# High part of the raw weight operands on VectorE instead of ScalarE, in fifteen pairs of a hybrid decoder layer

## The chip, the cores and the metric

The kernel runs on one core of one Trainium2 chip. The metric is device time in microseconds of one execution. Engines are named as in the profile: PE (TensorE matmuls) with PEld (its weight loads), DVE (VectorE), ACT (ScalarE), POOL (GpSimd) and SP, whose queue issues most of the DMAs. ACT and POOL issue some DMAs too.

## The reference

One layer over 1024 tokens of width 1024, in float32:

```
h = rmsnorm(x)
z_ssm, xBC, dt, q, k, v, f, z_att, g_ssm, g_att = split(h @ w_in)
A = chunked state-space scan over conv(xBC), gated by silu(z_ssm), group norm
B = causal attention with forgetting bias, times silu(z_att)
merged = sigmoid(g_ssm) * (A @ w_branch_ssm) + sigmoid(g_att) * (B @ w_branch_att)
out = x + rmsnorm(merged @ w_out)
```

The work of the matmuls is the four projections: `w_in` (9248 columns), the two branch matrices and `w_out`.

## The kernel before, in words

**Precision.** A float32 product is made of three matmuls on a rounded type: each operand is split into a high part (rounded) and a low part (what is left), and high x high, high x low and low x high are summed in PSUM. For weights this is `Pair.split`: the high part `op[:, 0]` is a copy with rounding, made by ACT (L355), and the low part `op[:, 1]` is source minus high part, made by DVE (L357). Both are 128 x 512 elements and lie in one buffer `wop`, of which there are four.

**Pairs.** The projections are done in units of 128 columns, two units at a time: a `Pair`. Its weights are four blocks `a11`, `a12`, `a21`, `a22` (unit, half of the 1024 rows), loaded by SP's DMAs into `raw` (six buffers, L348). The result of a pair comes from seven products of 12 matmuls each, in the manner of Strassen: steps 1, 2, 4 use a block as loaded (`a11`, `a12`, `a22`), steps 6, 5, 7, 3 use sums of blocks that DVE (POOL in some late pairs) adds first into `sum` (L364, L380) or back into `raw` (L388). So a name `wop<-raw` in the profile stands for steps 1, 2, 4, and for step 7 of those pairs that add in place. The other operands (`x0h`, `x0l` and so on) are blocks of the activations, split in the same way once per phase.

**What sets the order.** `Stream` holds one list of steps, and each call of `half` puts out half a step, 6 matmuls, on PE. The operand of a step is prepared three steps ahead (`ahead`). Results leave PSUM through ACT (L412, a copy that later steps add; L420) and DVE (L422, L424, L426). Around this run the other stages: the recurrence of four groups up to about 640 us, and attention from about 665 to 1130 us. Attention has 41 visits: scores (PE, tile `s`), row minimum with bias (DVE, L1558, into `ex`), exponential (ACT, L1563), transposes (PE, tile `pt`), copies out of PSUM (ACT L1602, DVE L1600), weighted sums (PE, tile `av`). At 24 places a small transpose `tp` (L133) follows, which waits for the first L1558 of its visit, since it takes the PSUM bank that this one reads. PE keeps the program's order exactly; on the other engines a scheduler places the instructions, and each engine then works through its own list in order. Marked calls (`pin`) keep their order.

**The pairs that the change touches** are `late` (four `za`, three `gs`, four `ga`: the gates of attention, of the recurrence's branch and of the attention branch) and `ends[:4]` (the products of the recurrence's branch with `w_branch_ssm`). They run from about 585 us to 1100 us, beside the end of the recurrence and most of attention.

## Time and profile before

| | us |
|---|---|
| median of 3 runs | 1289.95 (1289.72 to 1295.53) |
| the profiled execution's own time | 1288.93 |
| its span, first to last instruction | 1287.2 |
| PE busy | 1247.7 (97%) |
| DVE busy | 1018.2 (79%) |
| ACT busy | 796.8 (62%) |
| POOL busy | 285.8 (22%) |

PE is busy nearly all the time. Its matmuls overlap, so a busy PE may still lose a little between two of them. What the other engines do costs time only where PE has to wait for it, and such waits are listed by the profile's view of waits. A row of a group gives count, busy time, mean duration in ns, and the idle time of that engine just before the group's instructions with what ended it.

### The profile page before, as it was taken

What the parts mean: (1) busy time and instruction counts of PE and PEld (TensorE: products, weight loads), DVE (VectorE), ACT (ScalarE), POOL (GpSimd) and SP (SyncE); (2) the same over time, 40 slices, a digit from 0 to 9 for tenths busy, and PEclk for the clock granted to TensorE, in tenths of its full rate; (3) what the DMA queues carried; (4) which work ended last, traced back from release to release, by engine and by line L of the source; (5) the groups of instructions that cost most, each with busy time, mean ns of one, the idle gap of its engine ahead of it and who ended that gap; (6) DMA issues with size and microseconds to landing.
All of it is one profiled execution on the core that took longest, in us unless ns stands there. A gap on an engine that the chain in (4) does not pass through costs nothing.

```text
span 1287.2 us, 21110 instructions
## 1 busy us (share of the span) xinstructions
PE 1247.7 (97%) x7066; PEld 986.4 (77%) x7066; DVE 1018.2 (79%) x1979; ACT 796.8 (62%) x1728; POOL 285.8 (22%) x307
## 2 busy tenths in 40 slices
PE   6999999999999999899999999999999999999998
PEld 4787888788887888688777777777777777678886
DVE  6998888798789888788677766776778877976976
ACT  8745666566556656566556666666667656753753
POOL 0000330024102320134001222222111212346052
PEclk9999999999999999999999999999999999999999
DMA  7332543545363554545475664656587657665932
GB/s 282 100 107 71 159 143 125 195 140 151 131 188 122 151 175 145 142 131 152 149 256 173 214 215 163 238 197 210 193 279 279 219 187 248 238 210 198 369 114 101
DMA packets 154669, 233.60 MB, mean 181 GB/s; under 512 B 17216, under 2 KB 62656, under 8 KB 154560
## 3 DMA queue, kind: packets, MB, share of 16 engines
q1 hardware_dynamic: 142016, 205.53, 49.3%
q0 software_dynamic: 6400, 16.10, 3.3%
q10 hardware_dynamic: 6144, 10.62, 2.2%
q8 instruction: 56, 0.92, 0.3%
q14 instruction: 53, 0.43, 0.1%
HBM read 162.99 MB, written 72.34 MB: 183 GB/s over the span
## 4 chain that ended last, share of the span: by engine, by line
PE 62%; DVE 12%; DMA 9%; issue 7%; ACT 6%; SPq 2%; POOL 1%; ACTq 0%; DVEq 0%; POOLq 0%
PE pb L130 27%; PE pc L130 15%; PE pd L130 5%; PE pt L133 3%; PE av L130 3%; PE s L130 3%; DVE wop L357 3%; PE yps L130 2%; PE tr L133 1%; DVE ex L1558 1%; PE st L130 1%; ACT ex L1563 1%; ACT wop L355 1%; DMA xt<-in_x 1%; DVE sum L364 1%
## 5 line engine op out<-in xcount | busy, mean ns | idle before, releaser
L357 DVE TENSOR_TENSOR wop<-sum,wop 128x512 fp32r<-128x512 f32 x174 | 137.0, 789 | 59.5 <-ACT wop L355 59.1
L355 ACT ACTIVATE wop<-sum 128x512 fp32r<-128x512 f32 x174 | 108.8, 626 | 99.3 <-DVE sum L364 45.3
L1563 ACT ACTIVATE ex<-ex,nm 128x512 f32<-128x512 f32 (+1 forms) x192 | 116.0, 605 | 55.2 <-DVE nm L1558 54.8
L412 ACT ACTIVATE s<-pb 128x512 f32<-128x512 f32 x141 | 83.6, 593 | 101.8 <-PE pb L130 89.5
L357 DVE TENSOR_TENSOR wop<-raw,wop 128x512 fp32r<-128x512 f32 x149 | 114.5, 770 | 35.6 <-ACT wop L355 35.4
L130 PE MATMUL pc<-x3h,wop 128*128 128x512 f32 x384 | 131.2, 398 | 3.1 <-ACT wop L355 1.7
L130 PE MATMUL pb<-x0h,wop 128*128 128x512 f32 x384 | 132.6, 401 | 0.7 <-ACT x0h L1253 0.5
L130 PE MATMUL pc<-x2h,wop 128*128 128x512 f32 x384 | 131.8, 400 | 0.0
L130 PE MATMUL pb<-x5h,wop 128*128 128x512 f32 x376 | 128.0, 397 | 1.9 <-ACT s L412 1.9
L130 PE MATMUL pb<-x6h,wop 128*128 128x512 f32 x376 | 128.3, 397 | 1.1 <-ACT s L412 1.1
L130 PE MATMUL pb<-x4h,wop 128*128 128x512 f32 x376 | 127.6, 397 | 0.3 <-DVE wop L357 0.3
L1558 DVE CUSTOM_DVE_ANT_0 ex<-s,fb 128x512 f32<-128x512 f32 (+1 forms) x192 | 96.4, 552 | 12.2 <-PE s L130 12.1
L355 ACT ACTIVATE wop<-raw 128x512 fp32r<-128x512 f32 x151 | 94.0, 624 | 19.2 <-PE pc L130 11.2
L130 PE MATMUL pd<-x1h,wop 128*128 128x512 f32 x264 | 89.1, 396 | 0.0
L130 PEld LDWEIGHTS pc<-x3h,wop 128*128 128x128 f32 x384 | 72.1, 188 | 21.1 <-ACT wop L355 3.4
L130 PEld LDWEIGHTS pb<-x0h,wop 128*128 128x128 f32 x384 | 72.9, 190 | 17.4 <-ACT x0h L1253 1.5
L130 PEld LDWEIGHTS pc<-x2h,wop 128*128 128x128 f32 x384 | 72.1, 188 | 16.5 <-issue 1.5
L130 PEld LDWEIGHTS pb<-x5h,wop 128*128 128x128 f32 x376 | 70.6, 188 | 18.2 <-ACT s L412 3.0
L130 PEld LDWEIGHTS pb<-x6h,wop 128*128 128x128 f32 x376 | 70.6, 188 | 16.6 <-ACT s L412 1.5
L130 PEld LDWEIGHTS pb<-x4h,wop 128*128 128x128 f32 x376 | 70.5, 188 | 16.0 <-issue 0.7
L214 POOL TENSOR_TENSOR wd<-wd 128x256 f32<-128x256 f32 x32 | 31.7, 990 | 225.9 <-DMA wd<-in_wo 124.7
L130 PE MATMUL pb<-x0l,wop 128*128 128x512 f32 x192 | 75.7, 394 | 0.7 <-DVE x0l L1255 0.7
(341 smaller groups left out, 3000.9 us busy)
## 6 DMA issues: line engine op xcount, KB each, us to landing
raw<-in_wu SPq DMA_DIRECT2D x128, 256.0 KB, 3.7
csb<-cs_dram SPq DMA_DIRECT2D x32, 256.0 KB, 5.0
fb<-f_dram SPq DMA_DIRECT2D x16, 512.0 KB, 6.1
rb<-st_dram SPq DMA_DIRECT2D x48, 128.0 KB, 3.5
wd<-in_wo SPq DMA_DIRECT2D x40, 128.0 KB, 3.1
xt<-in_x SPq DMA_DIRECT2D x8, 512.0 KB, 5.9
gs_dram<-th ACTq DMA_DIRECT2D x16, 256.0 KB, 3.5
qh_dram<-th SPq DMA_DIRECT2D x16, 256.0 KB, 5.0
```

Source lines behind the costliest of these rows:

```text
L130: return tc.keep_in_program_order(nc.tensor.matmul(*args, **kw))
L133: return tc.keep_in_program_order(nc.tensor.transpose(out_, in_, idn))
L214: pin(nc.gpsimd.tensor_tensor(t[out_], t[a_], t[b_], ALU.subtract))
L355: nc.scalar.activation(op[:, 0], src, AF.Copy, scale=sign)
L357: nc.vector.tensor_tensor(op[:, 1], src, op[:, 0], ALU.subtract)
L364: self.adds.tensor_tensor(t, x, y, ALU.add)
L412: nc.scalar.activation(s, ps, AF.Copy)
L1558: nc.vector.tensor_tensor_reduce(to, bank(u, e), fb[hp, h][:, e, 0 : w[u]], 1.0, 3.0e38, ALU.add, ALU.min, nm)
L1563: nc.scalar.activation(to, to, AF.Exp, scale=-1.0, bias=nm, accum_out=hd.at(hd.sm, i, h, e))
```

## The change

In fifteen pairs (the eleven of `late` and `ends[:4]`) the high part of steps 1, 2 and 4 is made by a copy on DVE in place of the copy on ACT. That is 45 instructions of 128 x 512 elements that leave ACT and 45 that come to DVE; the low part stays on DVE, and everything else is as before.

```diff
@@ Pair.__init__
             self.raw, self.op, self.prepared = {}, {}, set()
+            self.alone = False
             self.s1, self.sums, self.closing = None, 0, None
@@ Pair.split
             with urgent:
-                nc.scalar.activation(op[:, 0], src, AF.Copy, scale=sign)
+                if self.alone and which in (1, 2, 4):
+                    nc.vector.tensor_copy(op[:, 0], src)
+                else:
+                    nc.scalar.activation(op[:, 0], src, AF.Copy, scale=sign)
                 if sign == 1.0:
                     nc.vector.tensor_tensor(op[:, 1], src, op[:, 0], ALU.subtract)
@@ after the list of pairs
     ends[-1].closing = closings[7]
+    for p in late + ends[:4]:
+        p.alone = True
```

The scheduler places the new copies and moves some neighbours. PE's and POOL's lists are the same as before. The changed file is longer, so its line numbers are higher by 4 to 6 from `split` on (the copy is its L357, the low part L361, the row minimum L1564).

The first place is DVE's list where attention's visit at 990 us begins, before:

```order
L364 TENSOR_TENSOR sum_10878<-raw_10529,raw_10531 128x512
L282 TENSOR_TENSOR x3l_10380<-x3l_10380,x3h_10379 128x512
L1600 COPY p_10705<-pt_10694 128x256
L282 TENSOR_TENSOR x3l_10380<-x3l_10380,x3h_10379 128x512
L1600 COPY p_10715<-pt_10696 128x256
L357 TENSOR_TENSOR wop_10665<-raw_10297,wop_10665 128x512
L422 TENSOR_TENSOR th_10668<-pc_10671,s_10462 128x512
L357 TENSOR_TENSOR wop_10726<-raw_10152,wop_10726 128x512
L1103 SCALAR_TENSOR_TENSOR th_10668<-th_10669,th_10668 128x512
L1558 ISA ex_6559,nm_10082<-s_10739,fb_10032 128x512
```

And with the change:

```order
L357 CAST wop_10665<-raw_10297 128x512
L368 TENSOR_TENSOR sum_10878<-raw_10529,raw_10531 128x512
L361 TENSOR_TENSOR wop_10665<-raw_10297,wop_10665 128x512
L282 TENSOR_TENSOR x3l_10380<-x3l_10380,x3h_10379 128x512 x2
L1606 COPY p_10705<-pt_10694 128x256
L1606 COPY p_10715<-pt_10696 128x256
L426 TENSOR_TENSOR th_10668<-pc_10671,s_10462 128x512
L357 CAST wop_10726<-raw_10152 128x512
L1107 SCALAR_TENSOR_TENSOR th_10668<-th_10669,th_10668 128x512
L361 TENSOR_TENSOR wop_10726<-raw_10152,wop_10726 128x512
L1564 ISA ex_6559,nm_10082<-s_10739,fb_10032 128x512
```

The operand `wop_10665`, copy and low part, now stands ahead of the two `x3l` rows; the copy of `wop_10726` stands between them and the row minimum.

The second place is the same list some 15 us later, ahead of the next row minimum, before:

```order
L364 TENSOR_TENSOR sum_10880<-sum_10878,raw_10297 128x512
L388 TENSOR_TENSOR raw_10297<-raw_10297,raw_10529 128x512
L357 TENSOR_TENSOR wop_10882<-sum_10880,wop_10882 128x512
L357 TENSOR_TENSOR wop_10965<-raw_10299,wop_10965 128x512
L380 TENSOR_TENSOR sum_10880<-sum_10880,raw_10299 128x512
L1558 ISA ex_6559,nm_10901<-s_10907,fb_10689 128x512
```

And with the change:

```order
L368 TENSOR_TENSOR sum_10880<-sum_10878,raw_10297 128x512
L392 TENSOR_TENSOR raw_10297<-raw_10297,raw_10529 128x512
L357 CAST wop_10965<-raw_10299 128x512
L361 TENSOR_TENSOR wop_10882<-sum_10880,wop_10882 128x512
L361 TENSOR_TENSOR wop_10965<-raw_10299,wop_10965 128x512
L384 TENSOR_TENSOR sum_10880<-sum_10880,raw_10299 128x512
L1564 ISA ex_6559,nm_10901<-s_10907,fb_10689 128x512
```

One row more stands ahead of the row minimum, and nothing has left.

The third place is SP's queue near 977 us, with what each DMA waits for (DMAHW0 to DMAHW7 are eight lanes that the DMAs take in turn; a DMA waits for the one before it on its lane), before:

```order
L1684 DMA x_10691<-t1_a_124 128x512 [waits DMAHW3_49,DMASW0_49]
L1397 DMA q_10683<-qh_dram_87 128x256 [waits DMAHW4_49,PE_49]
L1397 DMA q_10683<-ql_dram_88 128x256 [waits DMAHW6_49]
L1404 DMA k_10686<-kh_dram_89 128x512 [waits DMAHW7_49]
L1404 DMA k_10686<-kl_dram_90 128x512 [waits DMAHW0_49]
L1406 DMA fb_10689<-f_dram_78 128x2x512 [waits DMAHW1_49,DVE_49]
L348 DMA raw_10729<-in_wbs 128x512 [waits DMAHW2_49,Activation_49]
```

And with the change:

```order
L1690 DMA x_10691<-t1_a_124 128x512 [waits DMAHW3_49,DMASW0_49]
L349 DMA raw_10729<-in_wbs 128x512 [waits DMAHW5_49,DVE_49]
L1403 DMA q_10683<-qh_dram_87 128x256 [waits DMAHW6_49,PE_49]
L1403 DMA q_10683<-ql_dram_88 128x256 [waits DMAHW7_49]
L1410 DMA k_10686<-kh_dram_89 128x512 [waits DMAHW0_49]
L1410 DMA k_10686<-kl_dram_90 128x512 [waits DMAHW1_49]
L1412 DMA fb_10689<-f_dram_78 128x2x512 [waits DMAHW2_49,DVE_49]
```

The load of the weight block stands ahead of the loads of `q`, `k` and `fb`, and lane 2 is now that of `fb`.

## The prediction

> **What bounds the kernel now.** I read the page's first part, then the sums of the stage that the change touches (585 to 1102 us), then PE's waits there, and last the stretches of the timeline around those waits.

> ```profile
> span 1287.2 us, 21110 instructions
> PE 1247.7 (97%) x7066; PEld 986.4 (77%) x7066; DVE 1018.2 (79%) x1979; ACT 796.8 (62%) x1728; POOL 285.8 (22%) x307
> ...
> core 0: us, PE busy (x) PEld busy (x) DVE busy (x) ACT busy (x) POOL busy (x), PEclk, DMA share, GB/s
> 585.00:1102.00 517.00, 507.97 (x3333) 393.31 (x3333) 382.85 (x904) 329.67 (x786) 109.20 (x143) 1.00 0.63 210
> ```

> PE sets the end. In these 517 us it is idle for 517.00 - 507.97 = 9.0 us, and that is the most that anything on DVE and ACT can give back here, except for what overlapping matmuls hide. DVE has 134 us free (74% busy), ACT 187 us (64%). What PE waits for, in the same stretch (total, times, longest):

> ```profile
> PE tp L133 <- DVE nm L1558: 4.7, 6, 1.7
> PE pb L130 <- ACT s L412: 1.2, 1, 1.2
> PE s L130 <- ACT p L1602: 1.0, 1, 1.0
> PE pt L133 <- ACT ex L1563: 0.9, 3, 0.3
> PE s L130 <- DVE p L1600: 0.6, 1, 0.6
> ```

> No row names a weight operand: none comes late. Over half of the idle time is one place, the small transpose `tp`, which needs the first row minimum L1558 of its visit. So the question is whether DVE reaches that L1558 earlier or later.

> **The change part by part.** Removed from ACT are 45 copies, added to DVE are 45 (fifteen pairs, steps 1, 2, 4). The groups in the same stretch, the number of DVE's waits from the view of the tile `raw` (total, times), and the two nearest rows for a copy on DVE, over the whole run:

> ```profile
> L355 ACT ACTIVATE wop<-raw 128x512 fp32r<-128x512 f32 x61 | 38.2, 626 | 12.3 <-PE pc L130 11.2 <-PE pd L130 1.1
> ...
> L357 DVE TENSOR_TENSOR wop<-raw,wop 128x512 fp32r<-128x512 f32 x61 | 53.7, 881 | 32.6 <-ACT wop L355 32.6
> ...
>   ACT wop L355: 32.6, 24
> ...
> L1243 DVE TENSOR_SCALAR xt<-xt,rstd 128x512 f32<-128x512 f32 x2 | 0.9, 482 | 0.0
> ...
> L1600 DVE COPY p<-pt 128x512 f32<-128x512 f32 x32 | 21.9, 683 | 5.9 <-PE pt L133 5.9
> ```

> ACT loses 45 x 0.626 = 28 us. PE's waits on ACT (L412, L1602, L1563) total 3.1 us, and none follows one of the removed copies directly, so I count nothing for it; half of it at best would be 1.5 us.

> The copy's price on DVE lies between two rows: 0.482 us (one source, SBUF to SBUF) and 0.683 us (a copy, but out of PSUM). The new one has one source and both ends in SBUF, so I take 0.48. Rows on DVE overlap by 0.08 to 0.09 us (below, L357 at 1006.89 and the next row but one at 1008.10: two rows of 0.69 take 1.21), which leaves 0.40 in line, or 0.60 at the upper end. [...] No run here shows this copy with the rounded type as its result.

> 45 x 0.40 = 18 us come to DVE, against 32.6 us in which it stood idle before 24 of the 61 such low parts (45 of them change), waiting for ACT's copy. Where it stood idle, the copy goes into the wait. The clearest case is the visit at 817.88, ACT's rows, then DVE's, then PE's:

> ```profile
> 818.04 0.60 ACT L412 ACTIVATE s<-pb 128x512 f32<-128x512 f32 x1
> 818.52 0.64 ACT L355 ACTIVATE wop<-raw 128x512 fp32r<-128x512 f32 x1
> ...
> 819.19 0.69 DVE L357 TENSOR_TENSOR wop<-raw,wop 128x512 fp32r<-128x512 f32 x1 [1.20 <-ACT wop L355]
> 819.80 0.68 DVE L1558 CUSTOM_DVE_ANT_0 ex<-s,fb 128x512 f32<-128x512 f32 x1
> ...
> 819.60 0.87 PE L130 MATMUL av<-p,v 128*64 128x256 f32 x8
> 820.55 0.27 PE L133 MATMUL tp<-ident,ns 128*8 128x128 f32 x1
> ```

> DVE is free from 819.19 - 1.20 = 817.99; ACT first does L412. A copy on DVE could run at once and L1558 come 0.7 us earlier. PE gains only the gap between 820.47 and 820.55: **-0.08 us**. That is the pattern of most visits: what DVE gains lies ahead of work that PE wasn't waiting for.

> Where DVE had no idle time, a copy pushes L1558 back by 0.40. It costs PE time only where L1558 already came last. Three places have both. The first is the visit at 665 us, where PE waits for exponentials that follow L1558:

> ```profile
> 667.79 0.69 DVE L357 TENSOR_TENSOR wop<-sum,wop 128x512 fp32r<-128x512 f32 x1
> 668.40 0.69 DVE L357 TENSOR_TENSOR wop<-raw,wop 128x512 fp32r<-128x512 f32 x1
> ...
> 669.60 0.68 DVE L1558 CUSTOM_DVE_ANT_0 ex<-s,fb 128x512 f32<-128x512 f32 x1
> ...
> 671.90 0.33 PE L133 MATMUL pt<-ident,ex 128*128 128x128 f32 x1 [0.34 <-ACT ex L1563]
> ```

> The copy stands ahead of the first of these rows: **+0.40**. The second place is 988 to 1009 us, the two pieces of DVE's list that the section on the change shows:

> ```profile
> 989.44 0.69 DVE L282 TENSOR_TENSOR x3l<-x3l,x3h 128x512 fp32r<-128x512 f32 x1 [3.19 <-ACT x3h L281]
> ...
> 991.32 0.68 DVE L357 TENSOR_TENSOR wop<-raw,wop 128x512 fp32r<-128x512 f32 x1
> ...
> 993.72 0.68 DVE L1558 CUSTOM_DVE_ANT_0 ex<-s,fb 128x512 f32<-128x512 f32 x1
> ...
> 983.30 0.39 PE L130 MATMUL pb<-x4h,wop 128*128 128x512 f32 x1
> ...
> 994.46 0.27 PE L133 MATMUL tp<-ident,ns 128*8 128x128 f32 x1 [0.89 <-DVE nm L1558]
> ...
> 1006.89 0.69 DVE L357 TENSOR_TENSOR wop<-raw,wop 128x512 fp32r<-128x512 f32 x1
> ...
> 1008.10 0.68 DVE L1558 CUSTOM_DVE_ANT_0 ex<-s,fb 128x512 f32<-128x512 f32 x1
> ...
> 1008.85 0.27 PE L133 MATMUL tp<-ident,ns 128*8 128x128 f32 x1 [1.67 <-DVE nm L1558]
> ```

> The first operand (L357 at 991.32) moves into the 3.19 us of idle time before 989.44: its buffer was last read by the product whose last matmul starts at 983.30 (four buffers, four operands back). So 0.60 leaves the run of work ahead of 993.72 and one copy (0.40) enters: -0.20 at 994.46. Before 1008.10 another copy enters: +0.40. Together **+0.20**. The 3.19 us themselves come from ACT, whose store waited for the weight load on lane 2 of the DMAs:

> ```profile
> 988.29 0.60 ACT L412 ACTIVATE s<-pb 128x512 f32<-128x512 f32 x1 [3.90 <-DMA raw<-in_wbs]
> ```

> That load now goes out ahead of `q`, `k` and `fb`, but lane 2 is then that of `fb`, which is issued last and is no smaller, so I expect the same wait and count nothing. The third place is the visit at 1057:

> ```profile
> 1057.08 0.69 DVE L422 TENSOR_TENSOR th<-pc,s 128x512 f32<-128x512 f32 x1 [0.97 <-DMA ms_dram<-th]
> 1057.74 0.69 DVE L357 TENSOR_TENSOR wop<-raw,wop 128x512 fp32r<-128x512 f32 x1
> 1058.95 0.68 DVE L1558 CUSTOM_DVE_ANT_0 ex<-s,fb 128x512 f32<-128x512 f32 x1
> ...
> 1059.70 0.27 PE L133 MATMUL tp<-ident,ns 128*8 128x128 f32 x1
> ```

> Here ACT made its copy beside L422; now it follows on DVE: **+0.40**. It is so at other places behind L422 too (ACT's 12.3 us of waits for PE before these copies are theirs), but there `tp` has room. The copy waits for PE's release of its buffer in DVE's queue; L422 ahead of it waits for the same product, so nothing new is held up.

> Sum: -0.08 + 0.40 + 0.20 + 0.40 = **+0.9 us** (with 0.60 per copy: -0.08 + 0.60 + 0.60 + 0.60 = +1.7). The profiled execution took 1288.93, so 1289.8 by this; the median of the runs shown stands 1.0 above it, which gives 1290.9, say **1291**. The bounds of the sum alone, with half of PE's waits on ACT gained at one end, are 1289 to 1292.

> **Rivals.**

> *A. PE's waits go away.* For it: 32.6 us of DVE's waits and 28 us of ACT's work vanish, and 8.4 us of PE's idle time hang on these two engines. Against it: the clear case above gives PE 0.08, the waits ahead of most late L1558 aren't waits for a removed copy, and the longest of them (1.67) gets a copy more ahead of it. Half of it gives 1290 - 4.2 = 1285.8, all of it 1281.6. Chance 0.17.

> *B. VectorE becomes the bound: slower.* It is the busier of the two (79% against 62%). 37 of the 61 low parts found no wait, by share 37/61 x 45 = 27 of the copies. If each of these pushed PE by its price, as happens from the point where DVE has no idle time left in a visit, that is 27 x 0.40 = 11 us, or 16 at 0.60: 1301 to 1306. Against it are DVE's 134 free us. [...] By the trace DVE is not saturated in the mean. Chance 0.09.

> *C. Copies meet POOL.* Some low parts are stretched while POOL works:

> ```profile
> 802.93 3.24 DVE L357 TENSOR_TENSOR wop<-raw,wop 128x512 fp32r<-128x512 f32 x1
> ...
> 803.08 1.30 POOL L1649 TENSOR_TENSOR y<-y,zr 128x512 f32<-128x512 f32 x1
> 804.33 1.29 POOL L214 TENSOR_TENSOR x<-x,th 128x512 f32<-128x512 f32 x1
> ```

> The group's mean, 881, is 0.19 us above the undisturbed 690. The same for 45 copies is 9 us on DVE, of which by the share of critical places (4 of 24) and some luck 2 to 4 reach PE: 1293 to 1295. Against it: a copy that takes the collision spares the low part behind it. [...] Chance 0.14.

> **How the numbers follow.** The forecast has 0.58, A 0.17, C 0.14, B 0.09, and 0.02 are left for what I don't see. A measurement of this kernel tells a change from none at about 0.5%, 6.4 us: faster means under 1283.5, slower over 1296.4. Only the upper third of A is faster: 0.05. Slower is B and the tail of C: 0.10. The range, 1286 to 1297, leaves out A's better half and B.

> **What would show it.** Right: copies of 0.40 to 0.50 us; the row "DVE wop L357 <- ACT wop L355" loses over half of its time in this stretch; PE's idle time there stays within 8 to 11 us, with `tp` near 1009 us the longest wait. Wrong: copies of 0.68, or stretched to over 1 us in most visits; PE's waits on L1558 grow in number past ten (B); or the 1.2 us behind L412 are gone, when the DMA lane did matter.

## The result, and the profile after

| | before | after |
|---|---|---|
| median (22 runs each) | 1291.34 us (1287.41 to 1296.62) | 1295.71 us (1291.58 to 1300.48) |
| ratio after / before, 95% interval | | 1.0033 [1.0023, 1.0043] |
| the profiled execution's own time | 1288.93 | 1297.97 |

The change made the kernel slower by about 4.3 us. That is under the 0.5% that the prediction took as the bound, and inside its range of 1286 to 1297. The direction is certain nevertheless, and the size is about five times the sum of +0.9. (The forecast of 1291 stood on a median of three runs, 1289.95; on the median of 22 runs the same sum gives 1292.2.)

The first part of the page of the kernel after, then its sums between 585 and 1102 us:

```profile
span 1296.0 us, 21080 instructions
PE 1252.3 (97%) x7066; PEld 988.1 (76%) x7066; DVE 1032.0 (80%) x2024; ACT 771.9 (60%) x1683; POOL 288.8 (22%) x307
...
core 0: us, PE busy (x) PEld busy (x) DVE busy (x) ACT busy (x) POOL busy (x), PEclk, DMA share, GB/s
585.00:1102.00 517.00, 503.52 (x3299) 389.93 (x3296) 389.21 (x931) 299.63 (x727) 104.81 (x137) 0.99 0.63 208
```

ACT is busy for 24.9 us less over the span, DVE for 13.8 us more. PE's idle time in this stretch went from 9.0 to 517.00 - 503.52 = 13.5 us, above the 8 to 11 that the prediction allowed, and PE is also busy for longer over the span with the same 7066 matmuls (1252.3 against 1247.7). Over half of the second lies in the stretch at half clock that item 3 below counts: PE is busy there for 5.57 us with work that took 3.08 before. PE's waits in the same stretch (total, times, longest):

```profile
PE tp L133 <- DVE nm L1564: 6.3, 7, 2.0
PE pt L133 <- ACT ex L1569: 2.7, 3, 1.3
PE pb L130 <- ACT s L416: 1.5, 1, 1.5
PE s L130 <- DVE p L1606: 1.5, 2, 1.1
...
```

The waits for exponentials (`pt`) went from 0.9 to 2.7 us, still three of them: all lie in the visit at 665 us. How far PE is behind itself, instruction by instruction (start after minus start before), shows where the time went. When that visit begins it is 1.37 us, and first scores lie anywhere between 664.7 and 667.0 us in the profiles below whether or not the kernel loses, so I don't count this. In the next visit's scores the shift is 6.0 to 6.1 us. From there to 1067 us it grows by only 1.7 us more, to 7.8, and by 1102 us it is 9.1. These are two single executions, the one before 2.4 us under its kernel's median and the one after 2.3 us over it, so not all of these 9.1 us belong to the change.

The visit at 665 us in the timeline after, DVE's rows, then ACT's, then PE's:

```profile
667.27 0.69 DVE L675 SCALAR_TENSOR_TENSOR th<-th 128x512 f32<-128x512 f32 x1 [2.50 <-ACT th L674]
668.04 0.69 DVE L368 TENSOR_TENSOR sum<-raw 128x512 f32<-128x512 f32 x1
...
670.10 0.42 DVE L357 CAST wop<-raw 128x512 fp32r<-128x512 f32 x1
670.44 0.69 DVE L361 TENSOR_TENSOR wop<-sum,wop 128x512 fp32r<-128x512 f32 x1
...
672.25 0.68 DVE L1564 CUSTOM_DVE_ANT_0 ex<-s,fb 128x512 f32<-128x512 f32 x1
...
673.69 0.71 ACT L1569 ACTIVATE ex<-ex,nm 128x512 f32<-128x512 f32 x1
674.40 0.57 ACT L424 ACTIVATE th<-pb 128x512 f32<-128x512 f32 x1
674.87 0.62 ACT L359 ACTIVATE wop<-raw 128x512 fp32r<-128x512 f32 x1
675.39 0.60 ACT L1569 ACTIVATE ex<-ex,nm 128x384 f32<-128x384 f32 x1
...
666.70 0.97 PE L130 MATMUL s<-k,q 64*128 64x512 f32 x6
...
673.84 0.33 PE L133 MATMUL pt<-ident,ex 128*128 128x128 f32 x1 [1.04 <-ACT ex L1569]
...
676.14 3.21 PE L133 MATMUL pt<-ident,ex 128*128 128x128 f32 x12 [1.27 <-ACT ex L1569]
681.84 1.76 PE L130 MATMUL s<-k,q 64*128 64x512 f32 x12
```

And what answers to these rows in the kernel before, beside the ones that the prediction shows:

```profile
665.19 0.69 DVE L364 TENSOR_TENSOR sum<-raw 128x512 f32<-128x512 f32 x1 [1.78 <-DMA raw<-in_wu]
...
665.33 0.97 PE L130 MATMUL s<-k,q 64*128 64x512 f32 x6
...
672.50 0.33 PE L133 MATMUL pt<-ident,ex 128*128 128x128 f32 x1 [0.27 <-ACT ex L1563]
673.10 1.42 PE L133 MATMUL pt<-ident,ex 128*128 128x128 f32 x11 [0.27 <-ACT ex L1563]
...
675.85 1.65 PE L130 MATMUL s<-k,q 64*128 64x512 f32 x12
```

Counted from the visit's first scores (665.33 and 666.70), the next visit's scores begin at 10.52 and at 15.15 us. Three things make up these 4.6 us:

1. The row minimum stood at 4.27 us and stands at 5.55: +1.28. The first sum began at -0.14 and now begins at 1.34, since its weight block lands 1.35 us later. That gives +1.48. The product L675, which stood behind this sum, now runs in the wait ahead of it: -0.60. The copy adds 670.44 - 670.10 = 0.34, and the sums between follow each other a little less closely.
2. The third transpose stood at 7.17 and stands at 9.44: another +0.99. ACT does L424 and L359 between the second exponential and the third; before, they came after the fourth.
3. From the third transpose to the next visit's scores it was 3.35 us (PE busy for 3.08) and is 5.70 (5.57): another +2.35, with the same matmuls. The twelve transposes take 3.21 us here. Before, the same twelve took 673.10 + 1.42 - 672.50 = 2.02 us, with a wait of 0.27 in them.

The third goes with the granted clock, 1.00 before and 0.50 in all of the 5.70 us after. The same visit, in windows of 3.41 us whose bounds are those at which the granted clock changes (the column before the last two), after:

```profile
671.87:675.28 3.41, 1.58 (x7) 0.70 (x5) 2.63 (x9) 2.31 (x6) 0.00 (x0) 1.00 0.03 11
675.28:678.69 3.41, 2.42 (x10) 2.13 (x11) 1.97 (x3) 2.52 (x7) 0.00 (x0) 0.50 0.00 0
678.69:682.10 3.41, 3.41 (x12) 2.37 (x12) 0.26 (x2) 1.02 (x3) 0.00 (x0) 0.50 0.92 293
```

And before, windows of the same length over the same work:

```profile
670.70:674.11 3.41, 2.53 (x16) 1.71 (x15) 1.19 (x7) 3.41 (x11) 0.00 (x0) 1.00 0.00 0
674.11:677.52 3.41, 3.41 (x24) 2.33 (x24) 3.38 (x6) 2.95 (x6) 0.00 (x0) 1.00 0.23 77
```

After, PE was busy for 1.58 of 3.41 us (46%), and the clock was at half for the two windows that followed, 6.83 us; the second of them with PE busy all the time. Before, the emptiest window here was 74% busy and the clock stayed at 1.00.

### The profile page after: what moved, and what is told of

Its sections match the earlier page's. It is cut to its first block, busy times and chain, and to the rows that moved or that the text cites. A ratio compares the mean times of both kernels' runs of the same rounds, so it can differ in the third digit from the quotient of the medians.

```text
span 1296.0 us, 21080 instructions
## 1 busy us (share of the span) xinstructions
PE 1252.3 (97%) x7066; PEld 988.1 (76%) x7066; DVE 1032.0 (80%) x2024; ACT 771.9 (60%) x1683; POOL 288.8 (22%) x307
## 4 chain that ended last, share of the span: by engine, by line
PE 64%; DVE 14%; DMA 8%; issue 6%; ACT 6%; SPq 1%; POOL 1%; DVEq 0%; ACTq 0%; POOLq 0%
PE pb L130 27%; PE pc L130 16%; PE pt L133 4%; PE pd L130 4%; PE av L130 4%; PE s L130 4%; DVE wop L361 3%; PE yps L130 2%; DVE xs L809 1%; DVE sum L368 1%; DMA raw<-in_wu 1%; ACT ex L1569 1%; PE tr L133 1%; PE st L130 1%; DMA xt<-in_x 1%
## 5 line engine op out<-in xcount | busy, mean ns | idle before, releaser
L361 DVE TENSOR_TENSOR wop<-sum,wop 128x512 fp32r<-128x512 f32 x174 | 142.8, 822 | 56.8 <-ACT wop L359 56.3
L359 ACT ACTIVATE wop<-sum 128x512 fp32r<-128x512 f32 x174 | 108.8, 626 | 99.4 <-DVE sum L368 43.3
L416 ACT ACTIVATE s<-pb 128x512 f32<-128x512 f32 x141 | 83.5, 592 | 96.8 <-PE pb L130 85.3
L130 PE MATMUL pc<-x3h,wop 128*128 128x512 f32 x384 | 132.3, 401 | 3.9 <-ACT wop L359 2.0
L130 PE MATMUL pc<-x2h,wop 128*128 128x512 f32 x384 | 132.7, 402 | 0.0
L130 PE MATMUL pb<-x0h,wop 128*128 128x512 f32 x384 | 132.1, 400 | 0.6 <-ACT x0h L1259 0.5
L130 PE MATMUL pb<-x5h,wop 128*128 128x512 f32 x376 | 128.0, 397 | 2.2 <-ACT s L416 2.2
L130 PE MATMUL pb<-x6h,wop 128*128 128x512 f32 x376 | 128.2, 397 | 1.1 <-ACT s L416 1.1
L130 PE MATMUL pb<-x4h,wop 128*128 128x512 f32 x376 | 127.7, 397 | 0.3 <-DVE wop L361 0.3
L361 DVE TENSOR_TENSOR wop<-raw,wop 128x512 fp32r<-128x512 f32 x149 | 109.4, 737 | 18.9 <-ACT wop L359 17.5
L1564 DVE CUSTOM_DVE_ANT_0 ex<-s,fb 128x512 f32<-128x512 f32 (+1 forms) x192 | 96.1, 551 | 5.4 <-DMA rb<-st_dram 2.3
L130 PEld LDWEIGHTS pc<-x3h,wop 128*128 128x128 f32 x384 | 72.8, 190 | 22.0 <-ACT wop L359 3.8
L130 PE MATMUL pd<-x1h,wop 128*128 128x512 f32 x264 | 89.0, 395 | 0.0
L130 PEld LDWEIGHTS pb<-x0h,wop 128*128 128x128 f32 x384 | 72.5, 189 | 17.1 <-ACT x0h L1259 1.3
L130 PEld LDWEIGHTS pc<-x2h,wop 128*128 128x128 f32 x384 | 72.7, 189 | 16.6 <-issue 1.5
L130 PEld LDWEIGHTS pb<-x5h,wop 128*128 128x128 f32 x376 | 70.8, 188 | 18.6 <-ACT s L416 3.3
L130 PEld LDWEIGHTS pb<-x6h,wop 128*128 128x128 f32 x376 | 70.6, 188 | 16.6 <-ACT s L416 1.6
L130 PEld LDWEIGHTS pb<-x4h,wop 128*128 128x128 f32 x376 | 70.4, 188 | 16.5 <-DVE wop L361 1.1
L214 POOL TENSOR_TENSOR wd<-wd 128x256 f32<-128x256 f32 x32 | 29.9, 933 | 226.5 <-DMA wd<-in_wo 119.1
L130 PE MATMUL pc<-x3l,wop 128*128 128x512 f32 x192 | 75.7, 394 | 0.7 <-DVE x3l L282 0.7
L130 PE MATMUL s<-k,q 64*128 64x512 f32 (+3 forms) x576 | 73.1, 367 | 3.4 <-DVE p L1606 2.9
```

What stands on the lines that cost most here:

```text
L130: return tc.keep_in_program_order(nc.tensor.matmul(*args, **kw))
L214: pin(nc.gpsimd.tensor_tensor(t[out_], t[a_], t[b_], ALU.subtract))
L359: nc.scalar.activation(op[:, 0], src, AF.Copy, scale=sign)
L361: nc.vector.tensor_tensor(op[:, 1], src, op[:, 0], ALU.subtract)
L416: nc.scalar.activation(s, ps, AF.Copy)
L1564: nc.vector.tensor_tensor_reduce(to, bank(u, e), fb[hp, h][:, e, 0 : w[u]], 1.0, 3.0e38, ALU.add, ALU.min, nm)
```

## The experiments

The first question was where the time is lost, the second why the visit at 665 us tips, that is, falls to half clock. Each kernel ran on the same chip as runs of the kernel before. "The step at 665" is how much PE falls behind the kernel before between 664 and 700 us, in the profiled execution.

**Which pairs.** One kernel makes copies on DVE only in the four `za` pairs (12 copies), the other only in the other eleven (33).

```diff
-    for p in late + ends[:4]:
+    for p in late[:4]:               # e1_za
+    for p in late[4:] + ends[:4]:    # e2_rest
         p.alone = True
```

> The copies go to VectorE in the four za pairs alone (12 of the 45 copies, about 591 to 690 us); the other eleven pairs are as before. Theory 'place': most of the loss arises where attention begins, at 665 to 682 us, where VectorE's and ScalarE's lists changed their order and PE ran at a lower clock after a stall. Then this kernel loses nearly as much as the whole change: +3.5 to +6 us against before, and PE is about 4.5 us later at 690 us than before, as in the whole change. Theory 'load': each copy on VectorE costs about the same wherever it stands. Then the loss goes by the number of copies, 12/45 of 4.4 us: +1.2 us.

> The other part alone: the copies go to VectorE in the three gs and four ga pairs and in the four pairs of the recurrence's branch product (33 of the 45 copies, after 689 us); the four za pairs are as before, and the lists of VectorE and ScalarE at 665 to 682 us are those of the kernel before. Theory 'place': -0.5 to +1.2 us against before (the prediction's terms without the one at 665 us sum to +0.5). Theory 'load': 33/45 of 4.4 us: +3.2 us.

The twelve copies: 1.0034 [1.0019, 1.0049], step at 665 +3.02 us. The other 33: 1.0001 [0.9989, 1.0014], step -0.13. The whole loss belongs to the four `za` pairs, and 33 copies on DVE cost nothing that can be told from zero.

**Order of the neighbours.** The third kernel (e3) has all 45 copies, but holds the old order in this visit: the product L675 behind the first sum, and L424 and the high part of step 7 behind the exponentials. The fourth (e4) has no copy, and takes the other order in part: the product ahead of the first sum.

```diff
 # e3_held, beside the change
+                if self.held_order == 7:
+                    later[5, 1](pin)        # product and store of silu, unit 5, half 1
...
+    late[2].held_order, late[3].held_order = 4, 7   # pins L424; pins L359 of step 7 and the first sum
 # e4_swap, on the kernel before
+            order = pin if (dram, i, ch) == (za_dram, 5, 1) else lambda op: op
+            order(nc.vector.scalar_tensor_tensor(th, th, 1.0, t[ch], ALU.add, ALU.mult))
```

> The whole change, all 45 copies on VectorE, but at 665 to 682 us the order of before is kept: the first sum of blocks stands ahead of the product with the gate's tanh on VectorE, and ScalarE's four exponentials stand together ahead of the result's copy out of PSUM and the high part behind it. Theory 'place' in the form that the order costs: +0.3 to +1.5 us against before, PE is later by 0.4 to 1.4 us over that place in place of 4.7, and no stretch with a clock below 0.9 follows it. Theory 'place' in the form that the copy itself costs there: +3 us or more, with the stall of 2.7 us of PE left as it is in the whole change. Theory 'load': +4.4 us.

> The kernel before, with no copy moved; only the product with the gate's tanh is put ahead of the first sum on VectorE at 665 us, as in the changed kernel (ScalarE's list then has the result's copy and one high part ahead of the last of the four exponentials; in the changed kernel they stand ahead of the last two). Theory 'place, by the order': the first row minimum of the visit comes 0.7 to 1.3 us later, one exponential 1 us later, +1.5 to +4 us against before, the larger end if PE's clock falls after the stall. Theory 'load' and the theory that the copy itself costs there: 0 to +0.5 us.

With the old order held: 1.0031 [1.0015, 1.0047], step +1.77. With the product ahead and no copies: 1.0006 [0.9993, 1.0020], step +0.71. So the order alone is not the cause. In the third kernel the first sum was still late: DVE waited 3.27 us for its weight block, against 1.78 in the kernel before, and the sum began 1.35 us behind the first scores.

```profile
666.26 0.69 DVE L371 TENSOR_TENSOR sum<-raw 128x512 f32<-128x512 f32 x1 [3.27 <-DMA raw<-in_wu]
...
669.16:672.58 3.42, 1.89 (x10) 1.24 (x8) 3.42 (x9) 0.91 (x3) 0.00 (x0) 1.00 0.21 80
```

In its emptiest window PE was busy for 1.89 of 3.42 us, 55%, and in this execution the clock stayed at 1.00 behind it.

**Where the program lies in memory.** The page counts DMAs of the kind "instruction" (56 and 52 packets after the change). I took them to bring the engines the next stretch of their program, which is an estimate from their places in the trace of the kernel before: the 56 of 16 KB start 256 of PE's instructions apart in the mean, and of those of 8 KB some start about 128 of DVE's apart (behind 60, 189 and 317 of them, later behind 1085 and, at 652.70 us, behind 1215). The one that I took for PE's began 13.4 us ahead of the visit's first scores (at 653.33 us) in place of 8.6 (656.77). If that were the cause, instructions without use at the start of DVE's list would move the loss: 8 and 64 of them into the kernel before, 120 into the kernel after.

```diff
-    nc.vector.memset(eps4, 4.0 * EPS)
+    for _ in range(1 + 8):      # e5_pad8, on the kernel before; 64 in e7_pad64; 120 in e6, on the kernel after
+        nc.vector.memset(eps4, 4.0 * EPS)
```

> The kernel before, no copy moved, with eight more memsets of 128x1 on VectorE at the program's start, before its first work (0.03 us each in line; they write a constant again). They only move VectorE's instructions by eight places in its code, as the eight copies ahead of 650 us do in the changed kernel. Theory 'code loading': the trace shows 8 KB of VectorE's code being loaded at about 652.7 us in the kernels whose za pairs are as before, and 2 to 3 us earlier in the three kernels with copies in these pairs; in these three PE's 16 KB load then falls on the start of the loads of q, k and fb, and the weight blocks of the last za pair land 1.0 to 1.5 us later against PE. Then this kernel shows the same: VectorE's code load 14 to 15 us ahead of the first score matmul in place of 11.5 to 12.6, PE's 13 to 14 ahead in place of 7.4 to 8.6, the weight block's landing 0 to 0.6 us after it in place of 0.75 to 1.0 before it, and +1.5 to +4.5 us. Theories 'order', 'load' and 'price of the copy': 0 us (at most 0.3), and the loads stay where they were.

> The whole change with 120 more such memsets of 128x1 at VectorE's start: 120 and the eight copies ahead of 650 us make 128 places, which is how many VectorE instructions lie between two of its 8 KB code loads, so that the loads stand again where they were before. About 28 run while VectorE waits for the first tile of x, the others between its first instructions, at 0.03 us each (up to 0.5 us for PE). Theory 'code loading': the weight block lands again 0.7 to 1.0 us ahead of the first score matmul, PE's idle time from there to the next visit falls from 2.8 to under 1.9 us, and the time is 1.5 to 4 us under that of the whole change: +0.5 to +3 us against before. The other theories: +4.4 us and a little more.

> The kernel before with 64 more such memsets at VectorE's start: half of the 128 places between two code loads, so that none of VectorE's code loads falls near 650 us, but about 35 us earlier and later. If what matters is that VectorE's load at 652.7 us holds PE's back until the loads of q, k and fb are all under way (theory 'code loading', in the form that the kernel before profits from a chance), the weight block lands late as in the changed kernel: +1.5 to +4.5 us. If what hurts is VectorE's own load falling on the start of those transfers: 0 us, also if code loads don't matter at all.

Measured: 1.0002 [0.9989, 1.0015] with 8, 1.0001 [0.9984, 1.0017] with 64, 1.0044 [1.0028, 1.0059] with 120 on the kernel after. The steps at 665 were -0.51, +0.49 and +3.41. Shifting DVE's program neither brings the loss nor takes it away; this theory falls.

**Later loads.** The weight block of this visit stands behind the loads of `v` in SP's queue. This kernel (e8) is the one after with these two loads issued after the fourteen half steps in place of ahead of them.

```diff
         load_q(0, (5, 4))
-        for h in (1, 0):
-            load_v(0, h)
         for _ in range(14):
             stream.half()
+        for h in (1, 0):
+            load_v(0, h)
```

> The whole change, with the two first loads of v (512 KB) issued after the fourteen half steps ahead of attention's first visit instead of before them, so that the weight blocks of the last za pair come ahead of them in SP's queue; v is first read some 11 us after the first score matmul. VectorE's and ScalarE's lists change with it (the first sum then stands ahead of the evacuation before it). Theory 'late weight block' (whatever makes it late): the block lands over 1 us earlier against PE, the first row minimum comes 1 us earlier, PE's idle time there falls under 1.5 us, and the time is 1.5 to 4 us under that of the whole change. Theories 'load' and 'price of the copy': no gain over the whole change beyond 0.5 us.

1.0019 [1.0004, 1.0033], step +2.58. The first sum began in time again (-0.07 us from the first scores; its block landed 0.17 ahead of them, against 0.41 behind them after the change), but the row minimum still stood at 5.21, and there was half clock at this place. The late block is a part of the loss at most.

**One copy less, one copy alone.** The ninth kernel has all copies but that of step 2 of `late[2]`; the tenth has that one alone.

```diff
-                if self.alone and which in (1, 2, 4):
+                if self.alone and which in self.alone:
...
+        p.alone = (1, 2, 4)
+    late[2].alone = (1, 4)      # e9_but_one; e10_one: late[2].alone = (2,) and no other pair
```

> The whole change but for one copy: the high part of step 2 of the third za pair (made at 649.6 us, used by PE 11 us ahead of the first score matmul) stays on ScalarE; 44 copies on VectorE. With it PE's product of that step waits again for two engines, and the kernels without copies in the za pairs show a semaphore instruction of PE for it 12.5 us ahead of the first score matmul, which the five kernels with them lack; in these five PE's 16 KB of code are loaded 13.4 to 14.3 us ahead of that matmul instead of 7.3 to 8.6, where SP's issue of the first k load then takes 1.1 to 1.8 us and the weight block of the last za pair lands 1 us later. Theory 'PE runs ahead': the semaphore instruction is back, PE's code load is back at 7 to 9 us ahead, the block lands 0.4 to 1.1 us before the first score matmul, and the time is +0 to +1.5 us against before. Theory 'late by DVE's load' (it is the copies' own time on VectorE in these pairs, 44 of 45 still there): +4 us.

> The kernel before with only that one copy on VectorE (step 2 of the third za pair); VectorE's and ScalarE's lists at 665 us are those of the kernel with the product put ahead of the first sum, which cost nothing measurable (+0.2 us by the medians). Theory 'PE runs ahead': the semaphore instruction is gone, PE's code load comes 13 to 15 us ahead of the first score matmul, the weight block lands 0 to 0.6 us after it, PE is idle there for over 2 us in place of 0.9, and +2 to +4.5 us against before. Theory 'late by DVE's load': one copy of twelve, 0 to +0.4 us.

All but one: 1.0030 [1.0015, 1.0044], step +3.49. That one alone: 1.0024 [1.0008, 1.0040], step only +0.64. The theory that PE's load of program, coming early, makes the loss gave the ninth kernel +0 to +1.5 us; 1.0030 is +3.9 us, and at least +1.9 by its interval, so it falls too. Its rows at this place:

```profile
668.65 0.42 DVE L357 CAST wop<-raw 128x512 fp32r<-128x512 f32 x1
670.79 0.69 DVE L1565 CUSTOM_DVE_ANT_0 ex<-s,fb 128x512 f32<-128x512 f32 x1
...
672.12:675.53 3.41, 1.22 (x5) 0.66 (x6) 1.62 (x5) 3.41 (x11) 0.00 (x0) 1.00 0.00 0
675.53:678.95 3.42, 3.42 (x15) 3.13 (x14) 1.37 (x2) 1.60 (x4) 0.00 (x0) 0.50 0.47 153
```

The first scores began at 665.67, so the row minimum is at 5.12, PE is busy for 36% of a window, and the next one runs at half clock with PE full.

**Time on DVE without the change.** If DVE's lateness is enough, it needs no copy of a weight: the eleventh kernel is the one before with three copies of a score's bias on DVE, put ahead of the first row minimum of this visit (the values are overwritten by the row minimum). The twelfth has the change in all pairs but `late[2]` and `late[3]`, whose operands stand in this visit.

```diff
 # e11_three, on the kernel before
+                        if hp == g == n == u == e == 0:
+                            for _ in range(3):
+                                pin(nc.vector.tensor_copy(to, fb[hp, h][:, e, 0 : w[u]]))
 # e12_but_two_pairs
-    for p in late + ends[:4]:
+    for p in late[:2] + late[4:] + ends[:4]:
         p.alone = True
```

> The kernel before, no weight copy moved, with three extra copies of 128x512 on VectorE (fb into the tile that the row minimum then overwrites; 0.40 us each in line) right ahead of attention's first row minimum. ScalarE's list has the result's copy and one high part ahead of the second exponential, and the tanh ahead of the fourth, so the exponentials come another 1.0 to 1.7 us later. Theory 'stall and clock' (the loss is one place: the first row minimum comes late, PE waits there for over 2 us, and then runs at half clock for 3 to 7 us): PE's idle time at the place rises from 0.9 to 3 or 4 us, a stretch with a granted clock of 0.5 follows, and the time is 4 to 6 us over before, twice the stall. The same without the clock: +2.2 to +2.9 us and a clock of 1.0. Theory that the loss needs the moved weight copies (their load on VectorE, or the late weight block): +1.2 us or less.

> The whole change without the last two za pairs: 39 of the 45 copies on VectorE, none between 642 and 689 us but the three of other pairs; both lists at 665 us are those of before. Theory 'stall and clock': the first row minimum comes 4.0 to 4.5 us after the first score matmul as in the kernels without copies in the za pairs, no half clock follows, and the time is that of before, -0.5 to +1.2 us. Theory 'load': 39/45 of 4.4 us: +3.8 us.

The three copies: 1.0049 [1.0034, 1.0064], step +5.66, the largest of all. Its rows:

```profile
669.68 1.34 DVE L1559 COPY ex<-fb 128x512 f32<-128x512 f32 x3
671.15 0.69 DVE L1561 CUSTOM_DVE_ANT_0 ex<-s,fb 128x512 f32<-128x512 f32 x1
...
671.06:674.47 3.41, 0.53 (x3) 0.15 (x2) 2.96 (x9) 2.58 (x7) 0.00 (x0) 1.00 0.01 2
674.47:677.88 3.41, 2.64 (x10) 2.06 (x11) 1.03 (x2) 2.25 (x6) 0.00 (x0) 0.50 0.22 82
677.88:681.29 3.41, 3.41 (x13) 2.37 (x11) 0.36 (x1) 0.87 (x2) 0.00 (x0) 0.50 0.67 226
```

The copies take 671.15 - 669.68 = 1.47 us, the row minimum moves from 4.27 to 6.01, and PE's idle time and two windows of half clock make 5.66 of it. (The scheduler also put ACT's other work between the exponentials here, as after the change.) All pairs but two, 39 copies: 1.0004 [0.9994, 1.0015], step +0.39:

```profile
670.48 0.68 DVE L1564 CUSTOM_DVE_ANT_0 ex<-s,fb 128x512 f32<-128x512 f32 x1
...
671.48:674.89 3.41, 2.35 (x13) 1.36 (x13) 1.25 (x6) 3.41 (x11) 0.00 (x0) 1.00 0.00 0
```

**All of them side by side.** Row minimum and next scores are counted from the visit's first scores; PE's idle time is that between these two scores; the clock is the mean over the span of all runs of a kernel (for the kernel before, 107 runs beside the experiments).

| kernel | copies, where | ratio | row minimum | next scores | PE idle | half clock here | mean clock |
|---|---|---|---|---|---|---|---|
| before | 0 | 1 | 4.27 | 10.52 | 0.9 | no | 0.9973 |
| e5, 8 memsets | 0 | 1.0002 | 3.75 | 10.00 | 0.5 | no | 0.9972 |
| e7, 64 memsets | 0 | 1.0001 | 4.74 | 10.99 | 1.2 | no | 0.9968 |
| e4, product ahead | 0 | 1.0006 | 3.97 | 11.21 | 1.6 | no | 0.9974 |
| e2 | 33, not `za` | 1.0001 | 4.13 | 10.38 | 0.8 | no | 0.9967 |
| e12 | 39, not `late[2:4]` | 1.0004 | 4.66 | 10.90 | 1.1 | no | 0.9967 |
| e10 | 1, in `late[2]` | 1.0024 | 3.90 | 11.14 | 1.5 | no | 0.9966 |
| e8, `v` later | 45 | 1.0019 | 5.21 | 13.08 | 1.6 | yes | 0.9967 |
| e3, order held | 45 | 1.0031 | 6.03 | 12.28 | 2.4 | no | 0.9961 |
| e9 | 44 | 1.0030 | 5.12 | 13.99 | 2.5 | yes | 0.9952 |
| after | 45 | 1.0033 | 5.55 | 15.15 | 2.8 | yes | 0.9953 |
| e1 | 12, `za` | 1.0034 | 5.04 | 13.52 | 2.3 | yes | 0.9958 |
| e6, 120 memsets | 45 | 1.0044 | 5.24 | 13.91 | 2.6 | yes | 0.9956 |
| e11, three other copies | 0 | 1.0049 | 6.01 | 16.13 | 3.6 | yes | 0.9947 |

Every kernel whose row minimum stands past 5 us here is slower, and of the others only e10 is. In the profiled execution of e10 nothing at this place explains its 3 us: its emptiest window there was 55% busy and the clock stayed at 1.00. The clock may fall there in other executions, but its mean clock over all runs, 0.9966, is that of e2 and e12 (0.9967), which lose nothing that can be told from zero. So the loss of e10 stays open. The mean clock of all runs goes with the time: over the 157 runs of the thirteen changed kernels, 0.001 of it stands for 1.5 us (correlation -0.66). After is 0.0020 below before, so some 3 of its 4.3 us go with the clock. Inside the single kernels, their means taken out, 0.001 goes with 1.0 us (correlation -0.51), which would make it 2. A correlation over runs doesn't say which place tipped in each, and the mean clock does not sort the kernels by itself: e8 has that of e2 and e12, and is slower.

No version beats the kernel before. Of those that move copies, e2 and e12 equal it.

## Why the prediction was right, and which step failed

**The price of a copy: right.** The tile's view of the copies (least, median and most in ns):

```profile
L357 DVE CAST wop<-raw x44: 408/419/2625, 591.2 to 1082.5; 128x512 fp32r<-128x512 f32 x44
```

0.42 us, and 0.34 in line at 670.10, a little below the 0.48 and 0.40 that were taken from a row of another copy.

**Copies go into DVE's waits: right.** The group of low parts and DVE's waits for ACT in the same stretch, after:

```profile
L361 DVE TENSOR_TENSOR wop<-raw,wop 128x512 fp32r<-128x512 f32 x60 | 46.3, 774 | 15.3 <-ACT wop L359 14.2
L357 DVE CAST wop<-raw 128x512 fp32r<-128x512 f32 x44 | 21.5, 489 | 8.0 <-PE pb L130 7.8
...
DVE wop L361 <- ACT wop L359: 28.9, 19, 3.4
```

The 32.6 us of waits before low parts of raw blocks became 14.2, and 8.0 us of other waits moved ahead of the copies. The row named as a sign lost less than the forecast half, from 49.9 to 28.9 us, since it also holds the sums' low parts. The 39 copies outside two pairs cost 1.0004 [0.9994, 1.0015]: the sum for them was -0.08 + 0.20 + 0.40 = +0.5 us, and +0.5 was measured, with an interval from -0.8 to +1.9.

**The small terms: right in sign and near in size.** Of PE's rows that the prediction named, after:

```profile
1001.71 0.27 PE L133 MATMUL tp<-ident,ns 128*8 128x128 f32 x1 [0.65 <-DVE nm L1564]
1016.37 0.27 PE L133 MATMUL tp<-ident,ns 128*8 128x128 f32 x1 [1.93 <-DVE nm L1564]
1067.49 0.27 PE L133 MATMUL tp<-ident,ns 128*8 128x128 f32 x1 [0.40 <-DVE nm L1564]
...
995.80 0.60 ACT L416 ACTIVATE s<-pb 128x512 f32<-128x512 f32 x1 [4.04 <-DMA fb<-f_dram]
```

At the first, PE's shift against before falls by 0.24 (forecast -0.20: its wait goes from 0.89 to 0.65). At the second it grows by 0.26 (forecast +0.40: 1.67 becomes 1.93), at the third by 0.27 (forecast +0.40). In the clear case, the visit at 817.88, the row minimum came 826.36 - 825.18 = 1.18 us behind the first scores in place of 1.92, and PE's shift falls by 0.15 (forecast -0.08). The wait on DMA lane 2 stayed, now for `fb`, 4.04 us in place of 3.90, as expected. These are single executions, whose other stretches differ by a microsecond either way: the longest wait of `tp` is now 2.03 us at 785.01, where it was 0.98, and among all fourteen profiles it lies between nothing and 2.0 us there, behind the DMA `t_s<-th`.

**The term at 665 us: wrong, and as far as the runs can tell it is the whole miss.** It was put at +0.40, the price of one copy ahead of the row minimum. It measured +4.75 in the profiled execution, and between +2.6 and +3.5 in four other kernels with copies in these two pairs (+1.8 where the order was held, +0.6 with one copy alone). Three steps of the working failed there. It took DVE's run of work at this place to start when it did before, but its weight block lands 0.42 us after the first scores in place of 0.93 ahead of them, and the first sum starts 1.5 us later. Then it costed ACT's lost work at nothing and didn't look at ACT's order: with two of ACT's other instructions between the exponentials, another 1.0 us. Last, it took a wait of PE to cost its own length. Behind the idle time there (0.9 before, 2.8 after) the clock stood at 0.50 for 6.83 us, and PE took 2.35 us more for the same matmuls. Why the weight block lands later when copies stand in these pairs, I couldn't settle. After the change its load is issued 5.87 us ahead of the first scores in place of 6.08 and takes 6.28 us in place of 5.14; in the kernel with the order held it is issued at 4.57 and takes 5.19. Moving DVE's program did not bring the landing back. In e8 and e9 the block landed ahead of the first scores again (0.17 and 0.36 us), and both kernels are slower all the same.

**The rivals.** A, waits going away, did not come: PE's idle time grew. B had the sign and, in part, the mechanism (DVE without idle time, row minimum late), but counted 27 places by share at 0.40 each, 11 us; it was one place, at some 4 us, and e2 and e12 show the rest to cost nothing that can be told from zero. C came to 3 of 45 copies, no more: they took 1.16, 1.18 and 2.63 us against the median of 0.42, each beside an instruction of POOL. The longest:

```profile
809.94 1.29 POOL L1655 TENSOR_TENSOR y<-y,zr 128x512 f32<-128x512 f32 x1
810.13 2.62 DVE L357 CAST wop<-raw 128x512 fp32r<-128x512 f32 x1
811.18 1.28 POOL L214 TENSOR_TENSOR x<-x,th 128x512 f32<-128x512 f32 x1
```

Of the signs that would prove the forecast wrong, none came: no copies at 0.68, seven waits of `tp` on the row minimum in place of six, and the wait behind L416 still there. Of the three signs for it only the copies' duration came: the row of DVE's waits lost under half, and PE's idle time rose to 13.5 us, with the longest `tp` wait at 785 us. The signs looked at durations and waits in number, and missed the one place where a wait is multiplied.

**Luck.** That the range held the result was luck. Its part above 1292 was there for copies stretched by POOL, and 3 of 45 were; what filled it was the clock and the order at 665 us, which no term and no rival had.

## What to carry to other kernels

When work is moved to an engine with much free time, cost the places where that engine is already late one by one, and look at the order on the engine that gave the work up as well: here 39 of 45 copies cost about nothing, and the six in two pairs, by difference, 4 us. Here a wait of the matmul engine was not worth its length alone: with 2.8 us of idle time in place of 0.9, half clock followed for 6.83 us, and PE fell 4.75 us behind at this place in the profiled execution. Read the granted clock beside the waits (its stretches of half clock were 3.41 or 6.83 us long here), and look at more than one kernel: of the seven whose row minimum stands past 5 us at this place, six had half clock there in the profiled execution and one had none.

## What the hardware showed beyond this

A second place in e9, and the only such stretch in the profile of the kernel before, show that it isn't bound to this visit:

```profile
952.02:955.43 3.41, 1.97 (x14) 1.13 (x15) 3.38 (x7) 0.97 (x4) 1.61 (x3) 1.00 0.68 186
955.43:958.84 3.41, 3.41 (x17) 1.96 (x18) 3.02 (x12) 3.01 (x9) 0.00 (x0) 0.50 0.93 359
```

```profile
541.00:544.41 3.41, 0.61 (x5) 0.21 (x3) 3.15 (x5) 2.21 (x5) 1.30 (x1) 1.00 0.94 172
544.41:547.82 3.41, 3.41 (x10) 2.90 (x11) 3.41 (x8) 1.55 (x4) 0.65 (x1) 0.50 0.42 121
```

In both, PE was not idle all through the window ahead of half clock: it was busy for 1.97 and 0.61 us of the 3.41. The idle time of such a window was in two to four pieces at the visit at 665 us; at the other places it was mostly a single one, of 1.4 to 3.1 us.
